# The second norm's sums, roots and reciprocals, moved some early products later in a hybrid layer's MLP

## The chip, the core and the metric

The kernel runs on one core of a Trainium2 chip. A core has a matrix engine (TensorE, PE in the rows), a vector engine (VectorE, DVE), a scalar engine (ScalarE, ACT), a general engine (GpSimd, POOL) and DMA queues that SyncE (SP) issues. Each engine works through its own list of instructions in order and waits where an operand or a buffer isn't ready. The metric is the device time of one execution in microseconds, the median of several runs.

## The reference

One decoder layer on 1024 positions of width 1024, all in float32. The mixer (convolution and retention heads) comes first; the change lies in what follows it, the squared-ReLU MLP under the second RMS norm:

```python
def rms_norm(x, g, eps=NORM_EPS):
    xf = x.astype(jnp.float32)
    y = xf * lax.rsqrt(jnp.mean(xf * xf, axis=-1, keepdims=True) + eps)
    return (y * g.astype(jnp.float32)).astype(x.dtype)

def sq_relu_mlp(u, w_up, w_down):
    hdn = jax.nn.relu(u @ w_up)
    return (hdn * hdn) @ w_down

    h = h + hybrid_mixer(rms_norm(h, norm1_g), w_in, conv_w, conv_norm_g, ret_norm_g, w_out)
    h = h + sq_relu_mlp(rms_norm(h, norm2_g), w_up, w_down)
```

## The kernel before

Everything is held transposed: features on the 128 partitions, tokens along the row, in two halves of 512 tokens (`hs[0]`, `hs[1]`). A float32 product is made of three faster ones: both factors are rounded to a high part (hi, on ACT) and the rest (lo, `tensor_sub`, on DVE), and hi times hi, hi times lo and lo times hi are added in one PSUM bank (`mm`). A weight piece comes as `r` by DMA, and `split_piece` makes `wh` on ACT and `wl` on DVE from it.

The up product is done by quadrants, with seven products in the place of eight. `MLP_ORDER = (1, 2, 6, 5, 3, 7, 4)` is the order of the seven kinds: kind 1 multiplies the quadrant "11" of the scaled x, 2 the quadrant "21", 3 the quadrant "22", and 5, 6, 7, 4 the sums of quadrants t1, t2, t3, t4. Each product is 12 matmuls (four pieces of 128 rows, three each) into a bank, which `Pair.take` then adds to others: kind 1 is copied out (ACT), kind 2 makes the result quadrant "11", kind 3 makes "12", and so on.

The second norm does not wait for its own root: x times the gain goes into the products, and the reciprocal root `r` of each token is multiplied in later, in `Pair.put`, as max(c, 0) * r on DVE, which a square on ACT follows. So `r` is first needed for the quadrant "11", made from kinds 1 and 2. It comes about in these parts: the squares of x are summed over feature blocks in `sums_[0]`, `sums_[1]` (ACT squares, POOL adds, while the mixer's last products run); a column of ones on PE sums them over partitions into a bank of tokens by 4 (`token_rnorms`, 8 matmul rows); ACT takes the root (a table load goes ahead of it); DVE takes the reciprocal and copies each value over 128 columns (`wide`); and PE multiplies that by the identity, so that each token's value stands on all partitions of a bank of the pool `pn` (`spread`). 

Between the mixer and the main loop stand 14 early products, for two pairs p = 0, 1 of feature groups: the loop near the end of the function runs over `at` = 0 to 13, which this text calls step 0 to 13 with product 0 to 13 (0 and 1 are kind 1 for the two pairs, 2 and 3 kind 2, 4 and 5 kind 6 on t2, 6 and 7 kind 5 on t1), and after each product come the preparation of a later weight piece (`prepare`, four steps ahead), the rest of the operands by a list written out by hand (`rest[at]`: `put_hi`, `put_lo`, the sums `sum4`, and so on), the squares put off by a step (`put_now`), and `take`. Before the change the ones' sums, the roots and the reciprocals are written at step 1, the spreading at step 3, and the `take` of product 2 is put off to step 3, behind the spreading. Pair 0 has two PSUM banks in turn (pool `pm`), pair 1 four (`pr`). The order in the code is the order on each engine.

After the early products the main loop runs over 7 blocks in which up products and down products alternate; a down product takes `V`, the hi and lo parts of the squared quadrants (`v_split`; the lo part of the second pair is POOL's).

Of the kernel before, what the change touches and what calls it, by code (L numbers as in the profile page):

```python
# [70 lines left out]
def hybrid_layer(  # L71
# [18 lines left out]
    dve = Engine(nc.vector, 1.18, now, clock)  # L90
# [26 lines left out]
    def tmp():  # L117
        return temps[-1].tile([P, H], F32, tag="t", name=nm("t"))

    def bank(pool_=None):  # L120
        return (pool_ or pm).tile([P, H], F32, tag="b", name=nm("b"))
# [47 lines left out]
    def prepare(n=1):  # L169
        for _ in range(n):  # L170
            if plan:
                part = plan.pop(0)()
                if part is None:
                    part = plan.pop(0)()
                parts.append(part)
# [105 lines left out]
    for i, t in enumerate(ropes):  # L281
        nc.sync.dma_start(t, rope[i])

    def token_rnorms(sums_, r, pool_=None):

        n = r.shape[-1]
        b = bank(pool_ or pr)
        for c in range(n):
            for i, q in enumerate(sums_):
                nc.tensor.matmul(  # L290
                    b[:, c : c + 1], q[:, c * P : (c + 1) * P], ones,
                    start=(i == 0), stop=(i == len(sums_) - 1),
                )
        act.activation(r, b[:, :n], AF.Sqrt, bias=eps, scale=1.0 / D)
        dve.reciprocal(r, r)
        wide = []
        for c in range(0, n, 4):
            m = min(n - c, 4)
            d = tmp()[:, : m * P].rearrange("p (a b) -> p a b", b=P)
            dve.tensor_copy(d, r[:, c : c + m, None].to_broadcast([P, m, P]))  # L300
            wide += [d[:, j] for j in range(m)]
        return wide

    def spread(wide, pool_=None):

        b = bank(pool_ or pr)[:, : len(wide) * P]
        for c, d in enumerate(wide):
            nc.tensor.matmul(b[:, c * P : (c + 1) * P], d, ident, start=True, stop=True)
        return b
# [4 lines left out]
    rtok = cp.tile([P, NC_], F32, name="rtok")  # L314
    zr = xp.tile([P, NH, NC_], F32, name="zr")
    for half in range(2):
        vb = [bank(pr if half else pm) for _ in range(4)]
        for k in range(KT):
# [11 lines left out]
            if half == 1 and k == 3:  # L330
                for c, sl in ((0, hs[0]), (4, hs[1])):
                    b = bank(pm)
# [17 lines left out]
        for i in range(4):  # L350
            c = half * 4 + i
# [351 lines left out]
    def put_hi(name, j, src):  # L703
        u = unit(F32R, "U")
        act.copy(u[:, :H], src)
        U.setdefault(name, [None] * 4)[j] = (u[:, :H], u[:, H:])

    def put_lo(name, j, src, eng=dve):
        hi, lo = U[name][j]
        eng.tensor_sub(lo, src, f32(hi))  # L710
# [129 lines left out]
    pn = ctx.enter_context(tc.tile_pool(name="pn", bufs=2, space=PSUM))  # L840
# [47 lines left out]
    sums_ = [tmp(), tmp()]  # L888
# [29 lines left out]
    def source(name, j):  # L918
        return un[j][:, hi_ if name == "t3" else lo_]
# [56 lines left out]
    todo = {}  # L976
# [47 lines left out]
    def put_now():  # L1024
        fs, later[:] = list(later), []
        for f in fs:
            f()

    def add(a, b):
        t = tmp()  # L1030
        dve.tensor_add(t, a, b)
        return t

    r_half = [None, None]

    class Pair:

# [13 lines left out]
        def take(self, n, b):  # L1051
            if n == 1:
                self.acc = tmp()
                act.copy(self.acc, b)
            if n == 2:
                self.put("11", add(self.acc, b))
            if n == 6:
                dve.tensor_add(self.acc, self.acc, b)
            if n == 5:
                self.both = add(self.acc, b)  # L1060
            if n == 3:
                self.put("12", add(self.both, b))
            if n == 7:
                dve.tensor_add(self.both, self.both, b)
                self.put("22", self.both)
                dve.tensor_add(self.acc, self.acc, b)
            if n == 4:
                dve.tensor_add(self.acc, self.acc, b)
                self.put("21", self.acc)
# [30 lines left out]
    early = [Pair((pm, pr)[p]) for p in range(EARLY)]  # L1100

    def hi(name, *js):
        return [lambda j=j: put_hi(name, j, source(name, j)) for j in js]

    def lo(name, eng, *js):
        return [lambda j=j: put_lo(name, j, source(name, j), eng) for j in js]

    def call(f, *js):
        return [lambda j=j: f(j) for j in js]
# [4 lines left out]
    def lo22(j):  # L1114
# [1 line left out]

    rest = [
        todo[32] + lo("t2", dve, 0, 1) + hi("t2", 2) + call(hi22, 0, 1),
        todo[33] + lo("t2", dve, 2) + todo[34] + hi("t2", 3) + call(lo22, 0, 1) + call(hi22, 2, 3),
        lo("t2", dve, 3) + hi("t3", 3) + call(lo22, 2, 3),  # L1120
        call(sum4, 0, 1) + hi("t4", 0, 1) + lo("t3", dve, 3),
        call(sum4, 2, 3) + hi("t4", 2, 3) + call(fetch_back, 0, 1, 2),
# [9 lines left out]
    ]  # L1132
    for at, (n, p) in enumerate((n, p) for n in MLP_ORDER for p in range(EARLY)):
        b = early[p].product(n)
        if at == 1:
            wides = [token_rnorms([sums_[h]], rtok[:, 4 * h : 4 * h + 4]) for h in range(2)]
            up.fetch(4)
        if at == 3:
            r_half[:] = [spread(w, pn) for w in wides]
        prepare()  # L1140
        for f in rest[at]:
            f()
        put_now()
        if at == 2:
            b2 = b
            continue
        if at == 3:
            early[0].take(n, b2)
        early[p].take(n, b)

    def down_product(n, h):
        hi, lo = parts.pop(0)
# [30 lines left out]
    def jobs(b, old, new):  # L1183

        todo = []
        for k, n in enumerate(DOWN_ORDER):
            four = [[] for _ in range(4)]
            if k < 6:
                for j in range(2):
                    four[j].append(lambda n=DOWN_ORDER[k + 1], j=j: v_split(old, n, j))  # L1190
                    four[j + 1].append(lambda n=DOWN_ORDER[k + 1], j=j: v_next(old, n, j))
            elif b < NBLK - 2:
                for j in range(2):
                    four[j].append(lambda j=j: v_both(new, 1, j))
            if b == NBLK - 2:
                late = {4: ((0, "11"), (0, "21"), (0, "12"), (0, "22")), 5: ((1, "11"),)}.get(k, ())
                for f, x in zip(four, late):
                    f.append(lambda x=x: last_split(*x))
                if k == 6:
                    for q in range(4):  # L1200
                        x = x2[2 * q + 1]
                        four[q].append(
                            lambda x=x: pool.tensor_add(x[:, hs[0]], x[:, hs[0]], x[:, hs[1]])
                        )
                    for f, name in ((four[0], "12"), (four[2], "22"), (four[3], "21")):
                        f.append(lambda name=name: last_split(1, name))
            todo += four
        return todo
# [4 lines left out]
    for b in range(NBLK - 1):  # L1213
        new = [Pair(pm), Pair(pm)]
        todo = jobs(b, pairs, new)
# [46 lines left out]
    for sl in (slice(0, 512), slice(512, 768), slice(768, 1024)):  # L1262
        n = sl.stop - sl.start
        G = T // n
        out = []
        for i in range(KT):
# [34 lines left out]
            if i == 2 and last:  # L1301
                wide = token_rnorms(*last[0])
            if i == 3 and last:
                finish(wide, *last[1])
            elif finishing:
                finishing.pop(0)()
        last = ([ssq3[:, sl], sq], rtok[:, sl.start // P : sl.stop // P]), (sl, out)
    finish(token_rnorms(*last[0]), *last[1], end=True)
    while finishing:
        finishing.pop(0)()  # L1310
# [96 lines left out]
```

## Time and profile before

| | |
|---|---|
| median of 3 runs | 1109.75 us (1109.44 to 1110.27) |
| the profiled execution: its own time | 1111.85 us |
| its span | 1110.0 us |
| PE busy | 1065.7 us, 96% of the span |
| DVE busy | 926.0 us, 83% |
| POOL busy | 578.1 us, 52% |
| ACT busy | 454.2 us, 41% |
| mean granted clock of PE | 0.982 |

The span is the time from the first to the last instruction of one profiled execution; 1.85 us of that execution's own time lie outside it. The profiled execution is 2.1 us above the median of the runs. An engine's busy share is a mean over stages, and a matmul counts as busy at either clock.

### The profile page before, as it was taken

How to read it: one execution, taken by the hardware profiler on the slowest of the kernel's cores; microseconds unless marked ns; L12 is line 12 of the kernel's file. 1: busy time of each engine (PE TensorE's matmuls, PEld its weight loads, DVE VectorE, ACT ScalarE, POOL GpSimd, SP SyncE). 2: the span in 40 equal slices, each digit the busy share in tenths (PEclk: the TensorE clock that was granted, in tenths of full speed). 3: DMA queues.
4: the chain of work that ended last, by engine and by line, in shares of the span. 5: the costliest groups of instructions: out<-in, count | busy, mean ns of one | idle time of the engine just before them, and what ended most of it. 6: DMA issues, size and time to landing. Idle time of an engine off the chain costs nothing.

```text
span 1110.0 us, 13715 instructions
## 1 busy us (share of the span) xinstructions
PE 1065.7 (96%) x4872; PEld 883.4 (80%) x4872; DVE 926.0 (83%) x1171; ACT 454.2 (41%) x817; POOL 578.1 (52%) x393
## 2 busy tenths in 40 slices
PE   7999999998798799989999999999999999999997
PEld 6778888887586588867788888888888888888886
DVE  8786486689999845579999989989989899899945
ACT  8211431456236433354344343433443343434453
POOL 6253234437776323536827629448267286284553
PEclk9999999999899899989999999999999999999998
DMA  7311112130111523032131120221211201200204
GB/s 266 143 57 48 30 39 75 49 142 16 36 46 46 199 86 124 1 100 71 48 96 29 49 86 29 67 58 39 79 37 58 86 29 48 86 20 19 70 9 152
DMA packets 38868, 76.68 MB, mean 69 GB/s; under 512 B 4368, under 2 KB 6416, under 8 KB 38800
## 3 DMA queue, kind: packets, MB, share of 16 engines
q1 hardware_dynamic: 38800, 75.80, 21.1%
q8 instruction: 39, 0.64, 0.2%
q14 instruction: 29, 0.24, 0.1%
HBM read 70.02 MB, written 5.77 MB: 68 GB/s over the span
## 4 chain that ended last, share of the span: by engine, by line
PE 77%; DVE 14%; issue 3%; DMA 2%; ACT 2%; POOL 1%; SPq 0%; DVEq 0%; POOLq 0%; ACTq 0%
PE b L361 49%; PE b L1159 22%; DVE wl L65 3%; PE b L323 2%; DVE U L65 1%; DVE t L65 1%; DVE r L65 1%; DVE z L65 1%; DVE xs L65 1%; DMA wv<-w_v 1%; DVE x L65 1%; DVE cv L65 1%; POOL r L65 1%; PE b L570 1%; PE b L538 1%
## 5 line engine op out<-in xcount | busy, mean ns | idle before, releaser
L65 ACT CAST wh<-r 128x512 fp32r<-128x512 f32 x286 | 176.7, 620 | 385.0 <-PE b L361 204.0
L361 PE MATMUL b<-U,wh 128*128 128x512 f32 x992 | 310.5, 394 | 8.5 <-DVE z L65 3.6
L65 DVE TENSOR_TENSOR wl<-r,wh 128x512 fp32r<-128x512 f32 x257 | 240.2, 937 | 76.1 <-ACT wh L65 75.2
L65 POOL TENSOR_TENSOR r<-r,r 128x512 f32<-128x512 f32 x136 | 210.2, 1548 | 131.6 <-DVE wl L65 79.6
L1159 PE MATMUL b<-V,wh 128*128 128x512 f32 x784 | 242.3, 390 | 1.1 <-POOL V L65 1.1
L361 PEld LDWEIGHTS b<-U,wh 128*128 128x128 f32 x992 | 188.4, 190 | 50.2 <-issue 4.4
L65 DVE TENSOR_TENSOR x<-x,b 128x512 f32<-128x512 f32 (+1 forms) x320 | 198.1, 665 | 28.7 <-PE b L361 28.7
L361 PE MATMUL b<-U,wl 128*128 128x512 f32 x496 | 195.3, 394 | 0.0
L1159 PEld LDWEIGHTS b<-V,wh 128*128 128x128 f32 x784 | 147.0, 188 | 33.1 <-POOL V L65 1.9
L65 POOL TENSOR_TENSOR t<-t,t 128x512 f32<-128x512 f32 x70 | 106.8, 1530 | 101.5 <-ACT t L65 55.4
L1159 PE MATMUL b<-V,wl 128*128 128x512 f32 x392 | 152.5, 389 | 0.0
L361 PE MATMUL b<-uh,wh 128*128 128x512 f32 x320 | 107.0, 399 | 4.3 <-DVE z L65 4.3
L361 PEld LDWEIGHTS b<-U,wl 128*128 128x128 f32 x496 | 94.5, 191 | 19.9
L361 PE MATMUL b<-uh,wl 128*128 128x512 f32 x320 | 105.6, 395 | 1.9 <-DVE wl L65 1.9
L361 PE MATMUL b<-ul,wh 128*128 128x512 f32 x320 | 105.9, 396 | 0.7 <-DVE ul L65 0.7
L65 POOL TENSOR_TENSOR wl<-r,wh 128x512 fp32r<-128x512 f32 x29 | 39.3, 1356 | 98.2 <-ACT wh L65 92.7
L1159 PEld LDWEIGHTS b<-V,wl 128*128 128x128 f32 x392 | 73.6, 188 | 15.2
L65 POOL TENSOR_TENSOR V<-t,V 128x512 fp32r<-128x512 f32 x35 | 49.1, 1402 | 67.2 <-ACT V L65 67.2
L65 DVE TENSOR_TENSOR t<-t,b 128x512 f32<-128x512 f32 x112 | 76.1, 680 | 1.7 <-POOL t L65 1.2
L65 ACT ACTIVATE t<-t 128x512 f32<-128x512 f32 x64 | 40.3, 631 | 84.6 <-DVE t L65 83.9
L361 PEld LDWEIGHTS b<-uh,wh 128*128 128x128 f32 x320 | 60.2, 192 | 17.6 <-issue 4.5
L361 PEld LDWEIGHTS b<-uh,wl 128*128 128x128 f32 x320 | 61.0, 191 | 15.3 <-DVE wl L65 2.4
(155 smaller groups left out, 1505.1 us busy)
## 6 DMA issues: line engine op xcount, KB each, us to landing
r<-w_up_t SPq DMA_DIRECT2D x64, 256.0 KB, 2.6
r<-w_down_t SPq DMA_DIRECT2D x56, 256.0 KB, 2.6
r<-w_in_t SPq DMA_DIRECT2D x48, 256.0 KB, 2.6
xt<-xT SPq DMA_DIRECT2D x16, 256.0 KB, 5.4
xs<-xT SPq DMA_DIRECT2D x8, 512.0 KB, 6.2
r<-w_out_t SPq DMA_DIRECT2D x16, 256.0 KB, 2.6
x<-xT SPq DMA_DIRECT2D x8, 512.0 KB, 8.8
rope<-rope SPq DMA_DIRECT2D x6, 512.0 KB, 6.8
```

Of the source, the lines that this page charges most:

```text
L65: return f(out, *args, **kw)
L323: nc.tensor.matmul(vb[i], a[k][:, tsl], b[k // 2][:, vs], start=(k == 0 and a is uh and b is vh), stop=(k == KT - 1 and a is ul),)
L361: nc.tensor.matmul(b, a[:, k, :], rhs(n, k)[r], start=(start and i == 0), stop=(stop and i == len(ops) - 1),)
L538: nc.tensor.matmul(bs[:, j * P : (j + 1) * P], k[j][:, sl], q[j][:, sl], start=True, stop=True)
L570: nc.tensor.matmul(bo[:, js], vj, sc[:, js], start=True, stop=(S is None))
L1159: nc.tensor.matmul(b, a, r, start=(i == 0), stop=(i == len(ops) - 1))
```

## The change

`token_rnorms` is cut into `token_roots` (ones' sums and roots) and `rnorms` (reciprocals and copies). In the loop over the early products the ones' sums and roots stand behind the `take` of product 3, the reciprocals behind that of product 5, the spreading behind that of product 6. Product 2 is taken at its own step; `take` then only adds, and the multiplying with `r` (`put` of the quadrant "11", one for each pair) is kept in `waiting` and done at steps 7 and 8. `up.fetch(4)` moves from step 1 to step 0. In step 1 of `rest` the two scaled hi parts of the quadrant "22" go ahead of the operand t2 of the last row block.

```diff
-    def token_rnorms(sums_, r, pool_=None):
+    def token_roots(sums_, r, pool_=None):
...
         act.activation(r, b[:, :n], AF.Sqrt, bias=eps, scale=1.0 / D)
+        return r
+
+    def rnorms(r):
+
+        n = r.shape[-1]
         dve.reciprocal(r, r)
         wide = []
...
             dve.tensor_copy(d, r[:, c : c + m, None].to_broadcast([P, m, P]))
             wide += [d[:, j] for j in range(m)]
         return wide
+
+    def token_rnorms(sums_, r, pool_=None):
+        return rnorms(token_roots(sums_, r, pool_))
...
-    r_half = [None, None]
+    r_half, waiting = [None, None], []
...
             if n == 2:
-                self.put("11", add(self.acc, b))
+                c = add(self.acc, b)
+                if r_half[0] is None:
+                    waiting.append(lambda: self.put("11", c))
+                else:
+                    self.put("11", c)
...
-        todo[33] + lo("t2", dve, 2) + todo[34] + hi("t2", 3) + call(lo22, 0, 1) + call(hi22, 2, 3),
+        todo[33] + lo("t2", dve, 2) + todo[34] + call(hi22, 2, 3) + hi("t2", 3) + call(lo22, 0, 1),
...
         b = early[p].product(n)
-        if at == 1:
-            wides = [token_rnorms([sums_[h]], rtok[:, 4 * h : 4 * h + 4]) for h in range(2)]
+        if at == 0:
             up.fetch(4)
-        if at == 3:
-            r_half[:] = [spread(w, pn) for w in wides]
         prepare()
         for f in rest[at]:
             f()
         put_now()
-        if at == 2:
-            b2 = b
-            continue
+        early[p].take(n, b)
         if at == 3:
-            early[0].take(n, b2)
-        early[p].take(n, b)
+            roots = [token_roots([sums_[h]], rtok[:, 4 * h : 4 * h + 4]) for h in range(2)]
+        if at == 5:
+            wides = [rnorms(r) for r in roots]
+        if at == 6:
+            r_half[:] = [spread(w, pn) for w in wides]
+        if at >= 7 and waiting:
+            waiting.pop(0)()
```

In DVE's list before, the reciprocals and copies (`rtok`, `t_3720`, `t_3729`) stand between the operands of step 0 (`un_3540`, `U_3641`, `U_3643`) and the first row of step 1 (`wl_3740`):

```order
L65 TENSOR_TENSOR un_3540<-un_3540 128x512
L65 TENSOR_TENSOR U_3641<-un_3049,U_3641 128x512
L65 TENSOR_TENSOR U_3643<-un_3208,U_3643 128x512
L65 RECIPROCAL rtok<-rtok 128x4
L65 COPY t_3720<-rtok 128x512
...
L65 COPY t_3729<-rtok 128x512
L65 TENSOR_TENSOR wl_3740<-r_3402,wh_3739 128x512
```

In the changed list they stand behind steps 1 to 5; these are its rows of steps 4 and 5 up to the first row of step 6 (`wl_3879`), with the sums of quadrants `un`, the operands t4 (`U_3786`, `U_3788`), and the takes of products 4 and 5 (`t_3706`, `t_3739`):

```order
L65 TENSOR_TENSOR wl_3819<-r_3232,wh_3818 128x512
L65 SCALAR_TENSOR_TENSOR un_3376<-x_2982,sm,un_3376 128x512
L65 SCALAR_TENSOR_TENSOR un_3540<-x_2983,sm,un_3540 128x512
L65 TENSOR_TENSOR t_3706<-t_3706,b_3805 128x512
L65 TENSOR_TENSOR wl_3851<-r_3404,wh_3850 128x512
L65 TENSOR_TENSOR U_3786<-un_3049,U_3786 128x512
L65 TENSOR_TENSOR U_3788<-un_3208,U_3788 128x512
L65 TENSOR_TENSOR t_3739<-t_3739,b_3837 128x512
L65 RECIPROCAL rtok<-rtok 128x4
L65 COPY t_3860<-rtok 128x512
...
L65 COPY t_3863<-rtok 128x512
L65 TENSOR_TENSOR wl_3879<-r_3234,wh_3878 128x512
```

The first reciprocal thus moves 25 rows of operands, weights and takes further back: from straight behind `U_3643`, the last row of step 0, to straight behind `t_3739`, the take of product 5.

In PE's list before, the ones' sums stand behind product 1 (`b_3700`) and the spreading behind product 3 (`b_3782`), ahead of product 4 (`b_3823`):

```order
L361 MATMUL b_3700<-U_3560,wl_3613 128x512
L290 MATMUL b_3713<-ones,t_3013 128x1 x4
L290 MATMUL b_3722<-ones,t_3014 128x1 x4
L361 MATMUL b_3759<-U_3111,wh_3629 128x512 x2
...
L361 MATMUL b_3782<-U_3597,wl_3658 128x512
L308 MATMUL b_3795<-ident,t_3720 128x128 x4
L308 MATMUL b_3800<-ident,t_3729 128x128 x4
L361 MATMUL b_3823<-U_3641,wh_3681 128x512 x2
```

In the changed list the sums stand behind product 3 (`b_3766`) and the spreading behind product 6 (`b_3865`), ahead of product 7 (`b_3897`):

```order
L369 MATMUL b_3766<-U_3597,wl_3658 128x512
L290 MATMUL b_3793<-ones,t_3013 128x1 x4
L290 MATMUL b_3799<-ones,t_3014 128x1 x4
L369 MATMUL b_3805<-U_3641,wh_3689 128x512 x2
...
L369 MATMUL b_3865<-U_3696,wl_3755 128x512
L316 MATMUL b_3887<-ident,t_3860 128x128 x4
L316 MATMUL b_3892<-ident,t_3863 128x128 x4
L369 MATMUL b_3897<-U_3190,wh_3779 128x512 x2
```

The sums move past two products and the spreading past three; no matmul is added or taken away.

In ACT's list the table load and the two roots now stand behind the casts of t4 of step 3 (`U_3786`, `U_3788`) and ahead of the weight cast of step 4:

```order
L65 CAST wh_3779<-r_3406 128x512
L65 CAST U_3786<-un_3049 128x512
L65 CAST U_3788<-un_3208 128x512
...
L65 ACTIVATE rtok<-b_3793,eps 128x4
L65 ACTIVATE rtok<-b_3799,eps 128x4
L65 CAST wh_3818<-r_3232 128x512
L65 CAST U_3826<-un_3376 128x512
```

Before, they stood behind the copy of product 0 and ahead of the weight cast of step 1; the table load itself is the row ahead of the first root in either list.

## Rows read from the trace of the kernel before

**Rows 1.** The chain of work that ended last, from the profile page: its share of the span by engine.

```profile
PE 77%; DVE 14%; issue 3%; DMA 2%; ACT 2%; POOL 1%; SPq 0%; DVEq 0%; POOLq 0%; ACTq 0%
```

**Rows 2.** The timeline of TensorE (PE) alone from the first early product on: start us, length us, then what ran; in brackets the idle time before it and who ended it. L361 are products of the halves, L290 the sums by the column of ones, L308 the spreading by the identity matrix. A product is 12 matmuls; 494.87 and 497.59 are the first rows of products 7 and 8.

```profile
463.48 0.62 PE L361 MATMUL b<-U,wh 128*128 128x512 f32 x2
...
468.92 0.95 PE L290 MATMUL b<-ones,t 128*128 128x1 f32 x8
470.81 1.05 PE L290 MATMUL b<-ones,t 128*128 128x1 f32 x8 [0.95 <-POOL t L65]
471.73 0.71 PE L361 MATMUL b<-U,wh 128*128 128x512 f32 x2
...
477.28 1.95 PE L308 MATMUL b<-ident,t 128*128 128x128 f32 x16
478.98 0.71 PE L361 MATMUL b<-U,wh 128*128 128x512 f32 x2
...
484.38 0.80 PE L361 MATMUL b<-U,wh 128*128 128x512 f32 x1 [2.87 <-DVE U L65]
...
492.06 0.70 PE L361 MATMUL b<-U,wh 128*128 128x512 f32 x2 [1.36 <-DVE t L65]
...
494.87 0.62 PE L361 MATMUL b<-U,wh 128*128 128x512 f32 x2
...
497.59 0.62 PE L361 MATMUL b<-U,wh 128*128 128x512 f32 x2
```

**Rows 3.** The timeline of ScalarE (ACT) alone over the same stretch: a COPY takes a product's bank, a CAST of wh<-r rounds a weight piece.

```profile
474.21 1.28 ACT L65 ACT_TABLE_LOAD   x1
...
475.81 0.62 ACT L65 CAST wh<-r 128x512 fp32r<-128x512 f32 x1
...
481.92 0.56 ACT L65 COPY t<-b 128x512 f32<-128x512 f32 x1
482.38 0.62 ACT L65 CAST wh<-r 128x512 fp32r<-128x512 f32 x1
```

**Rows 4.** The timeline of VectorE (DVE) alone there. wl rows finish a weight piece, U rows the lo half of an operand, un rows make sums of quadrants, t rows that read b take a product's bank. The row of 500.62 is the first of step 6.

```profile
475.80 0.18 DVE L65 RECIPROCAL rtok<-rtok 128x4 f32<-128x4 f32 x1 [3.29 <-ACT rtok L65]
...
476.91 0.69 DVE L65 TENSOR_TENSOR wl<-r,wh 128x512 fp32r<-128x512 f32 x1
...
479.38 0.75 DVE L65 SCALAR_TENSOR_TENSOR un<-x,sm,un 128x512 f32<-128x512 f32 x1
480.04 1.41 DVE L65 SCALAR_TENSOR_TENSOR U<-x,sm,U 128x512 fp32r<-128x512 f32 x2
483.03 0.69 DVE L65 TENSOR_TENSOR wl<-r,wh 128x512 fp32r<-128x512 f32 x1 [1.58 <-ACT wh L65]
483.64 0.68 DVE L65 TENSOR_TENSOR U<-un,U 128x512 fp32r<-128x512 f32 x1
484.24 2.43 DVE L65 SCALAR_TENSOR_TENSOR U<-x,sm,U 128x512 fp32r<-128x512 f32 x2
...
487.20 2.43 DVE L65 SCALAR_TENSOR_TENSOR un<-x,sm,un 128x512 f32<-128x512 f32 x2
489.55 1.77 DVE L65 TENSOR_TENSOR U<-un,U 128x512 fp32r<-128x512 f32 x1
491.24 0.68 DVE L65 TENSOR_TENSOR t<-t,b 128x512 f32<-128x512 f32 x1
...
493.95 0.69 DVE L65 TENSOR_TENSOR wl<-r,wh 128x512 fp32r<-128x512 f32 x1
...
500.62 0.68 DVE L65 TENSOR_TENSOR wl<-r,wh 128x512 fp32r<-128x512 f32 x1
```

**Rows 5.** The timeline of GpSimd (POOL) alone there (r rows work on raw weight pieces, x rows on the running x).

```profile
483.80 1.66 POOL L65 TENSOR_TENSOR r<-r,r 128x512 f32<-128x512 f32 x1 [13.04 <-DVE wl L65]
487.36 1.72 POOL L65 TENSOR_TENSOR r<-r,r 128x512 f32<-128x512 f32 x1 [1.90 <-DVE wl L65]
489.04 1.73 POOL L65 TENSOR_TENSOR x<-x,x 128x512 f32<-128x512 f32 x1
```

**Rows 6.** The timeline of PE alone in the first block of the main loop, columns as in rows 2; L1159 are the down products. The row of 516.63 begins the first down product, those of 520.32 and 554.01 begin up products, that of 550.29 a down product.

```profile
516.63 0.62 PE L1159 MATMUL b<-V,wh 128*128 128x512 f32 x2
...
518.37 0.50 PE L1159 MATMUL b<-V,wh 128*128 128x512 f32 x1 [0.67 <-POOL V L65]
...
520.32 0.62 PE L361 MATMUL b<-U,wh 128*128 128x512 f32 x2
...
550.29 0.70 PE L1159 MATMUL b<-V,wh 128*128 128x512 f32 x2
...
554.01 0.70 PE L361 MATMUL b<-U,wh 128*128 128x512 f32 x2 [0.71 <-ACT t L65]
```

**Rows 7.** Busy time by stretch of the whole core: start and end, length, then PE, PEld (weight loads), DVE, ACT, POOL busy with their instructions, the granted clock of PE (1.00 is 2.4 GHz, 0.50 is 1.2 GHz), share and rate of the DMA engines.

```profile
371.00:377.90 6.90, 2.94 (x7) 2.39 (x8) 6.81 (x10) 3.38 (x7) 1.64 (x1) 0.51 0.50 156
...
484.38:490.70 6.32, 6.32 (x14) 4.46 (x14) 6.32 (x6) 1.66 (x3) 4.42 (x3) 0.51 0.67 182
...
498.00:554.00 56.00, 54.62 (x239) 44.35 (x239) 54.30 (x73) 21.84 (x40) 39.77 (x26) 1.00 0.20 66
557.00:1075.00 518.00, 517.44 (x2292) 427.92 (x2290) 476.02 (x664) 210.81 (x366) 293.13 (x196) 1.00 0.17 52
```

**Rows 8.** The timeline of PE alone at the end of its longest earlier wait after the start, columns as in rows 2.

```profile
374.96 0.76 PE L361 MATMUL b<-yh,wh 128*128 128x512 f32 x1 [6.68 <-DVE z L65]
```

## Prediction

> **What bounds the kernel now.** I read the chain of work that ended last, then PE's own timeline where the change lies, then the engines it waits for there, then the stretch behind.
>
> The chain gives PE 77% and DVE 14% of the span [rows 1]. PE's busy share can't grow much: between 557 and 1075 us it is busy for 517.44 of 518.00 us [rows 7]. What is won or lost ahead of 557 us therefore moves the end one for one, and the question is when PE reaches that stretch.
>
> In the early products PE's timeline shows four losses [rows 2]. Two products take 463.48 to 468.92, so one takes 2.72. The ones' sums occupy 468.92 to 471.73, 2.81 us, of which 0.95 is a wait for POOL's last addition; 1.86 is work. Product 4 stops until 484.38 (a wait of 2.87) for the lo part of t2's last operand, from DVE. Product 6 stops until 492.06 (1.36) for the bank of product 2, whose take was put off. The spreading takes 477.28 to 478.98, 1.70, with no wait. Product 7 starts at 494.87 and ends at 497.59.
>
> Why is DVE late? It waits 3.29 us for the roots, until 475.80 [rows 4], because ACT loads a table from 474.21 and can round the next weight only at 475.81 [rows 3]. From then on DVE trails PE: it takes product 5 just ahead of 500.62 [rows 4], when PE has finished product 7. In 498 to 554 us DVE is busy for 54.30 of 56.00 us [rows 7], and its delay costs PE two more losses there [rows 6]: 516.63 to 520.32 is 3.69 for one product, 0.97 too much (the lo part of V, from POOL, which is held up by DVE's weight piece), and 550.29 to 554.01 is 3.72, 1.00 too much (ACT, behind DVE's take).
>
> **The change part by part.** No row is added on any engine; the cost is in the order, so I lay the rows of before out anew, engine by engine, with their own durations.
>
> *Sums and roots, removed from step 1.* PE runs products 0 to 3 through and then sums: 463.48 + 4 x 2.72 + 1.86 = 476.22. The 0.95 wait is gone. ACT rounds the weight of step 1 in the place of the table load, 474.21 + 0.62 = 474.83, and DVE's first row of step 1 starts at 474.85 where it was 476.91 [rows 3, 4]: 2.06 earlier.
>
> *Step 1 and the operand of product 4.* DVE's second sum of quadrants ended at 479.38 + 0.75 = 480.13, 3.22 behind that first row; now it ends at 478.07. On ACT an operand's cast (about 0.5), the copy (0.46, from 481.92 to 482.38) and the weight's cast (0.62) follow [rows 3]: 479.65. So DVE's row of 483.03 starts at about 479.70, 3.33 earlier. The moved hi parts of "22" fill time in which ACT waits for DVE anyway; without that cover they are two casts, and they sat ahead of this weight before. The late operand is ready at 483.64 + 0.68 - 3.33 = 480.99 [rows 4], so PE still stops in product 4, finishes it at about 481.5 (two matmuls of 0.23 remain), and products 5 and 6 end at 486.95 (up to 2.7 later if the clock falls over this stop, which the next wait hides). The bank of product 2 is taken in time now, so the 1.36 goes.
>
> *Where the wait goes.* Behind product 6 PE has the spreading, and that needs the copies which stand in DVE's list behind the take of product 5. Everything on PE behind it is held: product 7 and all later ones. So when does DVE get there?
> - From 483.03 to 491.24 the same rows took 8.21. Their slow ones are slow beside POOL: two operand rows in 484.24 to 486.60 and two sums in 487.20 to 489.55 take about 2.35 a pair against 1.41 for the pair of 480.04, and the row of 489.55 lasts 1.77 against 0.68; POOL's rows of 483.80, 487.36 and 489.04 run at that time [rows 4, 5]. They follow DVE's weight pieces, so they move with them. With one take (0.60) put in: 479.70 + 8.21 + 0.60 = 488.51; the take of product 3 makes it 489.11.
> - ACT's table load stands now behind the second sum (489.55 + 0.08 - 3.33 + 0.60 = 486.90), an operand's cast (0.5), then load and roots (474.21 to 475.81, 1.60) and the weight (0.62): 489.62. DVE goes on at 489.65.
> - Eight rows of steps 4 and 5 follow. Before, the same eight took 493.95 to 500.62, 6.67, with a wait for ACT inside; ACT has two operand casts of t4 in front of the weight now, too, so I take the 6.67: 496.32. Uncontended they would be about 5.
> - Reciprocal and copy of the first half: the two halves took 475.80 to 476.91, 1.11, so about 0.65 to the first copy's end: 497.0.
>
> So PE waits from 486.95 to 497.0, ten us. Spreading (1.70) and product 7 (2.72) give 501.4.
>
> *The clock.* After the wait of 6.68 us that ended at 374.96 the granted clock was 0.51 over 371.00 to 377.90, that is 1.2 GHz for 2.9 us after PE went on; after the stop that ended at 484.38 it was 0.51 to 490.70, some 6.2 us [rows 7, 8]. At half the clock half of that is lost: 1.5 to 3.1 us, middle 2.3. In before it was hidden, since product 6 waited for the bank; here PE has nothing else to wait for and pays it. Product 7 ends at 503.7 against 497.59 [rows 2]: 6.1 later (5.3 to 6.9).
>
> *What comes back.* DVE does not lose as much: behind the copies it has a few rows of steps 6 and 7 and then waits for product 7. So it no longer trails PE, and the two losses of 0.97 and 1.00 [rows 6] go: 6.1 - 1.97 = 4.1. `up.fetch(4)` one step earlier costs nothing, as its pieces are first rounded at step 10; the deferred multiplications with r are needed by V at step 12 and by DVE alone, in the time that it waits for PE.
>
> The sum against the profiled execution is 1111.85 + 4.1 = 1115.95; that one lies 2.1 above the median, and I put the difference on the median: 1109.75 + 4.1 = 1113.9.
>
> *A rule against a row.* The table load lasts 1.28 us [rows 3]. The Trainium skill, page "ScalarE: Activation LUTs", Terms, gives about 2.7 us for copying a table set into the active tables. By that the roots' place on ACT would hold DVE 1.4 us more and the sum would be 5.5; by the row it stays at 4.1, and the row decides.
>
> **Bounds.** Downwards: DVE without any delay beside POOL or behind ACT: 25 rows from 474.85 at 0.61 (483.03 to 483.64) and 0.65 are 490.8; then product 7 ends at 497.5, level with before, and with both later losses gone the change is -2.1; with the clock's loss at 1.5, -2.9. Upwards: 6.9 with none of the later losses gone, and one us more for DVE: 7.9. I stand near the upper rows for DVE's path, since the same rows took that long beside the same POOL rows.
>
> **The rivals.**
> - *About level: DVE is partly freed.* POOL's rows could fall elsewhere, since DVE's takes of products 2 and 3 now lie singly between the others. If half of the five us of delay goes, the copy is ready at 494.5 and the change is +1.6: 1111.4. For it: such a take stands in the list between the rows that were slow beside POOL. Against it: POOL's rows follow DVE's weights and keep their distance. 0.20.
> - *Faster.* All of the delay goes: 1106.9 to 1107.7. It decides where the first copy ends at 492.9: from there 4.42 and 2.3 of clock reach 499.6, just the 1.97 that come back. That is four us ahead of my sum. If the clock also stays at 2.4 GHz the point is 495.1. 0.10.
> - *The later losses stay.* POOL and DVE are loaded as before in 498 to 554 [rows 7], and the V of the first down product may still come late: +6.1, 1115.9. Against it: DVE then has waited for PE for some us. 0.15.
> - *The forecast*, 1113.9, own range 1112.5 to 1115.5: 0.55.
>
> **How the numbers follow.** I count 0.2%, 2.2 us, as about what a measurement of this kernel can tell from no change. The forecast and the staying losses lie above it, 0.70; the level case lies within it, with a little of the others: 0.20; the rest, 0.10, is faster. The range reaches over the level case down to 1109.3 and up to 1117.3 (7.5 above, near the upper bound).
>
> **What would show it.** Right: one long wait of PE ahead of the spreading of about ten us, on DVE's copy, with the clock at 1.2 GHz behind it; a shorter stop in product 4, near two us; no wait ahead of product 6, and none in the first block of the main loop; DVE's reciprocals near 496. Wrong: the copy ending ahead of 493, the wait short, or PE at 2.4 GHz straight behind it; or stops in the first block as long as before.

## The result, and the profile after

The changed kernel takes 1114.68 us (median of 6 runs, 1113.4 to 1115.18) against 1110.25 us for the kernel before (6 runs, 1109.44 to 1110.54): ratio 1.0039, interval 1.0027 to 1.0052. That is 4.43 us slower (3.0 to 5.8 by the interval); 4.1 were forecast. The profiled execution has a time of 1114.82 and a span of 1113.0 us, 3.0 longer than the span of before. The profiled execution of before lay 1.6 above its median and this one 0.14, so this pair of traces shows 3.0 of the 4.43.

The chain that ended last, from the page after: PE's share rose from 77 to 82%, DVE's fell from 14 to 11% [rows 1].

```profile
PE 82%; DVE 11%; issue 3%; ACT 2%; DMA 0%; POOL 0%; SPq 0%; DVEq 0%; POOLq 0%; ACTq 0%
```

All waits of PE from 440 to 580 us of the kernel after: line, what it waited for, us in total, how often, the longest.

```profile
PE b L316 <- DVE t L65: 9.9, 1, 9.9
PE b L369 <- DVE U L65: 1.8, 1, 1.8
PE b L369 <- ACT U L65: 0.3, 1, 0.3
```

The same for the kernel before:

```profile
PE b L361 <- DVE U L65: 2.9, 1, 2.9
PE b L361 <- DVE t L65: 1.4, 1, 1.4
PE b L290 <- POOL t L65: 0.9, 1, 0.9
PE b L361 <- ACT t L65: 0.7, 1, 0.7
PE b L1159 <- POOL V L65: 0.7, 1, 0.7
```

Five waits, 6.6 us together, became three, 12.0 together. What stopped PE for the bank, for POOL's t, for V and for ACT's t is gone; in its place stands one wait of the spreading (L316) for DVE's copy. PE's timeline after, with the columns of [rows 2]; L369 are products of the halves:

```profile
463.09 0.62 PE L369 MATMUL b<-U,wh 128*128 128x512 f32 x2
...
473.97 1.84 PE L290 MATMUL b<-ones,t 128*128 128x1 f32 x16
...
480.62 0.50 PE L369 MATMUL b<-U,wh 128*128 128x512 f32 x1 [1.83 <-DVE U L65]
...
496.74 3.78 PE L316 MATMUL b<-ident,t 128*128 128x128 f32 x16 [9.89 <-DVE t L65]
500.17 0.82 PE L369 MATMUL b<-U,wh 128*128 128x512 f32 x2
...
503.12 0.62 PE L369 MATMUL b<-U,wh 128*128 128x512 f32 x2
```

The row of 503.12 is the first of product 8, and so the end of product 7. Product 0 starts 0.39 us earlier than in before (463.09 against 463.48), ahead of all that the change moves, so 0.39 is added where places of the two are compared. But for the two stops in product 4 (0.3 and 1.8 us in the list of waits), sums and products 4 to 6 follow each other up to 486.85, then PE stands for 9.89 us.

DVE's timeline after, over the wait, with the columns of [rows 4]:

```profile
484.03 2.44 DVE L65 SCALAR_TENSOR_TENSOR un<-x,sm,un 128x512 f32<-128x512 f32 x2
486.40 1.76 DVE L65 TENSOR_TENSOR U<-un,U 128x512 fp32r<-128x512 f32 x1
...
489.40 1.65 DVE L65 TENSOR_TENSOR wl<-r,wh 128x512 fp32r<-128x512 f32 x1 [0.64 <-ACT wh L65]
...
493.58 0.76 DVE L65 TENSOR_TENSOR wl<-r,wh 128x512 fp32r<-128x512 f32 x1 [0.61 <-ACT wh L65]
...
496.06 0.16 DVE L65 RECIPROCAL rtok<-rtok 128x4 f32<-128x4 f32 x1
496.26 0.43 DVE L65 COPY t<-rtok 128x512 f32<-128x512 f32 x1
...
503.81 0.69 DVE L65 TENSOR_TENSOR wl<-r,wh 128x512 fp32r<-128x512 f32 x1 [4.78 <-ACT wh L65]
```

But for two waits of 0.6 us for ACT, DVE works until its first copy ends at 496.69; 0.05 later PE starts. Behind the copies DVE runs out of work and stands for 4.78 us: it no longer trails PE. The busy times by stretch after, with the columns of [rows 7]:

```profile
486.70:496.74 10.04, 0.15 (x2) 0.00 (x1) 8.76 (x13) 4.91 (x9) 5.07 (x4) 0.67 0.54 195
496.74:500.20 3.46, 3.46 (x17) 3.46 (x17) 2.25 (x5) 0.00 (x0) 0.39 (x1) 0.50 0.50 192
500.20:503.00 2.80, 2.80 (x14) 2.34 (x14) 0.00 (x0) 0.00 (x0) 2.80 (x3) 0.96 0.03 10
503.00:557.00 54.00, 54.00 (x240) 44.72 (x239) 49.60 (x68) 22.40 (x40) 35.68 (x24) 1.00 0.14 39
```

The spreading runs at 0.50, 1.2 GHz, and takes 3.43 us (496.74 to 500.17) where it took 1.70 in before; product 7 is back at 2.4 GHz all but its start (0.96) and takes 2.95 (500.17 to 503.12) in the place of 2.72. From 503 to 557 PE is busy all the time.

### The profile page after: what moved, and what is told of

Read it like the earlier page. It is cut to its first block, busy times and chain, and to the rows that moved or that the text cites. A ratio compares the mean times of both kernels' runs of the same rounds, so it can differ in the third digit from the quotient of the medians.

```text
span 1113.0 us, 13717 instructions
## 1 busy us (share of the span) xinstructions
PE 1063.8 (96%) x4872; PEld 883.0 (79%) x4872; DVE 926.2 (83%) x1171; ACT 454.3 (41%) x817; POOL 576.6 (52%) x393
## 4 chain that ended last, share of the span: by engine, by line
PE 82%; DVE 11%; issue 3%; ACT 2%; DMA 0%; POOL 0%; SPq 0%; DVEq 0%; POOLq 0%; ACTq 0%
PE b L369 53%; PE b L1171 23%; PE b L331 2%; DVE wl L65 2%; DVE r L65 1%; DVE z L65 1%; DVE xs L65 1%; DVE U L65 1%; DVE cv L65 1%; DVE ul L65 1%; PE b L578 1%; PE b L546 1%; DVE un L65 1%; PE b L586 1%; PE b L580 1%
## 5 line engine op out<-in xcount | busy, mean ns | idle before, releaser
L369 PE MATMUL b<-U,wh 128*128 128x512 f32 x992 | 308.5, 392 | 5.7 <-DVE z L65 3.6
L65 DVE TENSOR_TENSOR wl<-r,wh 128x512 fp32r<-128x512 f32 x257 | 237.4, 927 | 84.1 <-ACT wh L65 82.7
L369 PEld LDWEIGHTS b<-U,wh 128*128 128x128 f32 x992 | 187.5, 189 | 46.2 <-issue 2.3
L369 PE MATMUL b<-U,wl 128*128 128x512 f32 x496 | 194.2, 391 | 0.0
L369 PE MATMUL b<-uh,wh 128*128 128x512 f32 x320 | 107.0, 399 | 4.4 <-DVE z L65 4.3
L369 PEld LDWEIGHTS b<-U,wl 128*128 128x128 f32 x496 | 93.8, 189 | 19.8
L369 PE MATMUL b<-uh,wl 128*128 128x512 f32 x320 | 105.7, 395 | 1.9 <-DVE wl L65 1.9
L369 PE MATMUL b<-ul,wh 128*128 128x512 f32 x320 | 105.9, 396 | 0.7 <-DVE ul L65 0.7
L369 PEld LDWEIGHTS b<-uh,wh 128*128 128x128 f32 x320 | 60.2, 192 | 17.6 <-issue 4.5
L369 PEld LDWEIGHTS b<-uh,wl 128*128 128x128 f32 x320 | 61.0, 191 | 15.3 <-DVE wl L65 2.4
L369 PEld LDWEIGHTS b<-ul,wh 128*128 128x128 f32 x320 | 60.9, 190 | 14.6 <-DVE ul L65 1.6
```

The lines of the kernel that those rows point to most:

```text
L65: return f(out, *args, **kw)
L369: nc.tensor.matmul(b, a[:, k, :], rhs(n, k)[r], start=(start and i == 0), stop=(stop and i == len(ops) - 1),)
```

## The experiments

The theory: PE waits for copies that stand late in DVE's list; what this costs is the wait, plus the slow clock behind it, less the later losses that vanish since DVE is no longer behind. The first rival: it is the new order on DVE (takes, multiplications with r) that costs the time, wherever the spreading stands. The second: the clock costs little, and the wait alone is the loss. E1 to e4 ran together (before: 1109.97 us there), and e5 to e8 (before: 1109.9).

**e1: the spreading two products later, all else as in the changed kernel.**

```diff
+        if at == 8:
+            r_half[:] = [spread(w, pn) for w in wides]
         early[p].take(n, b)
 ...
-        if at == 6:
-            r_half[:] = [spread(w, pn) for w in wides]
-        if at >= 7 and waiting:
+        if at >= 8 and waiting:
```

> The changed kernel with the spreading placed behind product 8 in the place of product 6 (ahead of that product's take, which needs r); DVE's reciprocals stay where the change put them. Theory (the loss is PE's wait ahead of the spreading for DVE's copy, at about 496.7): products 7 and 8 run inside that wait, delayed by 2.1 us and 1.3 us for the banks of products 3 and 4, the wait ahead of the spreading shrinks from 9.9 us to about 1 us, product 9 starts 1.5 to 1.9 us earlier than in the kernel before, and as DVE too is some 1.8 us ahead of before, the time is 1108.4 us (1107.5 to 1109.5), 6 us below the changed kernel and below the kernel before. Rival (the loss comes from DVE's and ACT's order, the late table load and the late takes): these stay, so the time stays near 1114.5.

Measured: 1108.81 us, ratio 0.9986 (0.9977 to 0.9995): 1.2 below the kernel before and, with each set against the kernel before that ran with it, 5.6 below the changed kernel. PE's timeline in e1, its four waits of over half a microsecond up to the spreading:

```profile
478.44 0.66 PE L369 MATMUL b<-U,wh 128*128 128x512 f32 x1 [1.82 <-DVE U L65]
...
486.74 0.70 PE L369 MATMUL b<-U,wh 128*128 128x512 f32 x2 [0.51 <-ACT rtok L65]
...
491.00 0.70 PE L369 MATMUL b<-U,wh 128*128 128x512 f32 x2 [1.26 <-ACT U L65]
494.65 2.05 PE L316 MATMUL b<-ident,t 128*128 128x128 f32 x16 [0.64 <-DVE t L65]
```

This execution runs 2.18 earlier than the one after (the stop in product 4 ends at 478.44 against 480.62), so its spreading starts at 496.83 in the times of after: the copies are as late as they were. PE has done products 7 and 8 in the meantime and waits 0.64 instead of 9.89. (The waits of 0.51 and 1.26 ahead of these two products are put down to ACT; by order and time they are for the banks of products 3 and 4, which DVE's takes free, as e8 shows for the second.) DVE's list is the same up to the copies, so the first rival falls: the place in PE's list is what costs.

**e2: the spreading where the change has it, on data that are there early** (it leaves out the scale of the second norm).

```diff
+    ready = [[ident] * 4] * 2
 ...
-            r_half[:] = [spread(w, pn) for w in wides]
+            r_half[:] = [spread(w, pn) for w in ready]
```

> The changed kernel with the spreading in its place behind product 6, but made from the identity matrix, which is ready from the start, in the place of DVE's copies; DVE still makes reciprocals and copies. So r is 1 and the second norm's scale is left out of the hidden values. Theory: PE has no wait ahead of the spreading; product 7 waits to 488.8 for the bank of product 3, product 8 to 493.0 for that of product 4, and from there DVE is the bound, which stands where it does in the changed kernel, some 1.8 us ahead of the kernel before: 1108.3 us (1107.3 to 1109.5). Rival (DVE's or ACT's order is to blame): 1114.5.

Measured: 1107.6 us, ratio 0.9981 (0.9972 to 0.9989). PE's timeline: the spreading has no wait, and others come back behind it.

```profile
488.17 1.95 PE L316 MATMUL b<-ident 128*128 128x128 f32 x16
...
494.69 0.70 PE L369 MATMUL b<-U,wh 128*128 128x512 f32 x2 [1.24 <-ACT U L65]
...
516.59 0.50 PE L1172 MATMUL b<-V,wh 128*128 128x512 f32 x1 [1.02 <-POOL V L65]
```

With PE not held, DVE is behind again, and the loss at the first down product is there, as in before [rows 6]. Both halves of the theory, the wait and what comes back, show in this one run.

**e3 and e5: matmuls without use ahead of the spreading**, 36 and 42 of them, to keep PE from standing.

```diff
         if at == 6:
+            warm = bank(pn)
+            for i in range(36):        # 42 in e5
+                nc.tensor.matmul(
+                    warm, U["11"][i % 4][0][:, :P], U["11"][i % 4][0], start=True, stop=True
+                )
             r_half[:] = [spread(w, pn) for w in wides]
```

> The changed kernel with 36 matmuls of 128x512 on an operand that is ready (about 8.2 us), into a bank of the pool pn, put between product 6 and the spreading, that is inside PE's wait of 9.9 us. Theory: the granted clock stays at 2.4 GHz, the spreading takes 1.7 us in the place of 3.4, and the time falls by that: 1112.9 us (1112.3 to 1113.6). Rival (the clock's part is nothing, or the spreading's 3.4 us come from its operands): 1114.6, no change against the changed kernel; if the matmuls overrun the wait, above 1114.6.

> As the kernel with 36 matmuls ahead of the spreading, with 42 of them (about 9.5 us), so that PE's wait behind them is about 0.4 us in the place of 1.9 us. Theory (the clock falls because PE waits, and costs 1.7 us in the spreading): the granted clock stays at 1.00 through the spreading, which takes 1.7 us, and the time is 1112.9 us (1112.3 to 1113.6) against about 1114.6 for the change. Rival (the spreading is slow for another reason): the spreading takes 3.3 us again at 0.5, and the time is 1114.6.

Measured: e3 1113.04 (ratio 1.0026, 1.0016 to 1.0035), e5 1112.44 (1.0021, 1.0012 to 1.0030). PE's timeline in e3, and then the busy times by stretch (columns of [rows 7]) over its spreading:

```profile
488.65 8.32 PE L1161 MATMUL b<-U 128*128 128x512 f32 x36
498.88 3.63 PE L316 MATMUL b<-ident,t 128*128 128x128 f32 x16 [1.91 <-DVE t L65]
```

```profile
498.88:502.30 3.42, 3.42 (x17) 3.42 (x17) 2.25 (x5) 0.00 (x0) 0.74 (x1) 0.53 0.71 224
```

In e3 1.91 us of wait are left, and the clock fell to 0.53 all the same; so this trace doesn't tell the clock from the wait. It is also of e3's slowest execution (1116.87), so that the median of 1113.04, as expected, is not explained by it. In e5 the matmuls reach over the copy. PE's timeline, DVE's first copy, and the busy times:

```profile
489.87 9.68 PE L1161 MATMUL b<-U 128*128 128x512 f32 x42
499.39 1.95 PE L316 MATMUL b<-ident,t 128*128 128x128 f32 x16
...
501.10 0.71 PE L369 MATMUL b<-U,wh 128*128 128x512 f32 x2
```

```profile
498.01 0.43 DVE L65 COPY t<-rtok 128x512 f32<-128x512 f32 x1
```

```profile
499.00:503.00 4.00, 4.00 (x27) 3.61 (x26) 1.78 (x3) 0.00 (x0) 2.78 (x3) 1.00 0.43 139
```

Here PE never stands behind product 6, the clock is 1.00, and the spreading takes 1.71 us (499.39 to 501.10) instead of 3.43: 1.7 us are the clock's, and the second rival falls. By the medians the clock's part is about 1.9 (e5 is 2.5 us slower than the kernel before, 1.3 to 3.3, and the changed kernel 4.4). This trace, of e5's slowest execution, shows less of that in the end (649.1 us from product 0 on, against 649.9 after), since its matmuls run 0.95 us over the copy's end at 498.44. The other 2.5 are what the wait costs with the clock kept up.

**e4: the kernel before, and in it only the take of product 2 put back in its turn.**

```diff
         if at == 2:
-            b2 = b
+            c2 = add(early[0].acc, b)
             continue
         if at == 3:
-            early[0].take(n, b2)
+            early[0].put("11", c2)
```

> The kernel before with one part of the change alone: the take of product 2 (the addition) at its own step 2; the multiplication with r stays behind the spreading at step 3. Theory (DVE is the bound from step 3 to 554 us, so a wait of PE taken away there comes back later): the wait of 1.36 us ahead of product 6 goes, but the waits at the first down product and at 554 us grow by as much: 1110.2 us, within 0.4 of the kernel before. Rival (PE's waits add up, each removed one is a gain): 1108.9.

Measured: 1110.26 us, ratio 1.0003 (0.9994 to 1.0012): no difference. PE's timeline in e4, at product 4 and at the start of product 8:

```profile
481.27 0.79 PE L361 MATMUL b<-U,wh 128*128 128x512 f32 x1 [2.85 <-DVE U L65]
...
493.85 0.74 PE L361 MATMUL b<-U,wh 128*128 128x512 f32 x2 [2.35 <-DVE t L65]
```

The 1.36 ahead of product 6 [rows 2] is gone, and 2.35 stands ahead of product 8, again for DVE's t. The time is as expected; the place is not: the wait comes back there and not at the first down product, whose 0.67 is gone too. While DVE is behind PE, a wait that is taken away came back at a later thing that DVE owes.

**e6: four of POOL's subtractions, `new_basis` 5 and 7, two and three steps later**, behind those that wait for a DMA.

```diff
-        call(new_basis, 5),
-        call(new_basis, 7),
-        call(new_basis, 3),
+        [],
+        [],
+        call(new_basis, 3),
+        call(new_basis, 5, 7),
```

> The changed kernel with POOL's four subtractions on the running x (new_basis 5 and 7) written at step 11 in the place of steps 8 and 9, so that they stand behind those of step 10, which wait for a transfer until about 499.8 us, and no longer run beside DVE's rows of steps 3 to 5. Theory (DVE's rows on two SBUF operands wait while POOL runs): the row of 1.76 us at 486.40 falls to 0.68, but DVE then waits for ACT's weight until 489.40 all the same; the row of 1.65 at 489.40 falls to 0.69 and the rest of steps 4 and 5 comes 1.0 us earlier; the first copy ends at 495.7 in the place of 496.7 and the time falls by 1.0 us, to 1113.6 (1112.9 to 1114.3). Rival (POOL's rows have no part in DVE's delay): 1114.6 and the same rows of DVE.

Measured: 1113.57 us, ratio 1.0034 (1.0021 to 1.0047). DVE's timeline in e6, with the rows that answer to those of 486.40 and 489.40 after, and PE's:

```profile
485.15 0.68 DVE L65 TENSOR_TENSOR U<-un,U 128x512 fp32r<-128x512 f32 x1
...
488.15 0.69 DVE L65 TENSOR_TENSOR wl<-r,wh 128x512 fp32r<-128x512 f32 x1 [1.72 <-ACT wh L65]
```

```profile
494.46 3.78 PE L316 MATMUL b<-ident,t 128*128 128x128 f32 x16 [8.91 <-DVE t L65]
```

Without POOL beside them the two rows last 0.68 and 0.69 instead of 1.76 and 1.65. Of these 2.04 us 1.08 go into a longer wait for ACT (1.72 instead of 0.64), and 0.98 reaches PE. So POOL does slow these rows, as the prediction had it, and about half of what they delay is hidden behind ACT. What the 0.98 are worth at the end is not settled: in this execution product 7 started at 1.2 GHz too (0.75 over 497.92 to 500.72), and from product 0 on the trace takes as long as the one after (650.0 us against 649.9); by the medians e6 is 0.8 closer to the kernel before than the changed kernel is, which is within their intervals.

**e7: reciprocals and copies one step earlier on DVE.**

```diff
-        if at == 5:
+        if at == 4:
             wides = [rnorms(r) for r in roots]
```

> The changed kernel with the reciprocals and copies one step earlier on DVE, behind the take of product 4; the spreading stays behind product 6. Theory (the end follows the time of DVE's first copy one for one as long as PE waits there): the copy ends at about 493.5 in the place of 496.7, PE's wait is 6.7 us in the place of 9.9, and the time is 1111.4 us (1110.7 to 1112.3). Rival (the loss hangs on the spreading's place in PE's list alone): 1114.6; rival (the later stretch takes up the gain): above 1113.

Measured: 1111.14 us, ratio 1.0011 (1.0002 to 1.0020). DVE's timeline in e7 at the first copy, POOL's beside it, and PE's at the wait:

```profile
492.52 0.98 DVE L65 COPY t<-rtok 128x512 f32<-128x512 f32 x1
```

```profile
491.95 1.26 POOL L65 TENSOR_TENSOR x<-x 128x512 f32<-128x512 f32 x1 [2.02 <-DVE un L65]
```

```profile
493.56 3.48 PE L316 MATMUL b<-ident,t 128*128 128x128 f32 x16 [7.33 <-DVE t L65]
```

The wait shrinks by 2.56 instead of 3.2: the copy lies now beside a row of POOL's and lasts 0.98 instead of 0.43. The time is as expected and neither rival's: as long as PE waits there, the end follows DVE's copy.

**e8: roots at step 2, reciprocals at step 3, spreading at step 7.**

```diff
-        if at == 3:
+        if at == 2:
             roots = ...
-        if at == 5:
+        if at == 3:
             wides = [rnorms(r) for r in roots]
-        if at == 6:
+        if at == 7:
             r_half[:] = [spread(w, pn) for w in wides]
```

> The changed kernel with sums and roots behind the take of product 2 (where ACT is idle), reciprocals behind that of product 3, the spreading behind product 7. Theory: the table load no longer holds DVE (0.64 us), PE finds the copies nearly ready (at about 489.4) and waits at most 0.3 us ahead of the spreading, then some 1.3 us for the bank of product 4; DVE is the bound to 554 us and stands 2.4 us ahead of the kernel before, and PE waits again in the first block: 1107.8 us (1106.8 to 1108.8), level with or just below the kernel with the spreading at step 8. Rival (PE's waits add up): 1105.5 or less.

Measured: 1106.9 us, ratio 0.9972 (0.9961 to 0.9982): 3.0 us faster than the kernel before and, each against its own kernel before, 7.4 faster than the changed kernel. PE's timeline in e8, and two rows of DVE's:

```profile
487.81 1.16 PE L316 MATMUL b<-ident,t 128*128 128x128 f32 x8 [0.16 <-DVE t L65]
489.22 1.16 PE L316 MATMUL b<-ident,t 128*128 128x128 f32 x8 [0.25 <-DVE t L65]
491.83 0.69 PE L369 MATMUL b<-U,wh 128*128 128x512 f32 x2 [1.46 <-ACT U L65]
...
513.05 0.50 PE L1171 MATMUL b<-V,wh 128*128 128x512 f32 x1 [0.99 <-POOL V L65]
```

```profile
487.87 1.29 DVE L65 COPY t<-rtok 128x512 f32<-128x512 f32 x1
...
491.01 0.67 DVE L65 TENSOR_TENSOR t<-t,b 128x512 f32<-128x512 f32 x1
```

The spreading waits 0.41 us in all. The 1.46 ahead of product 8 are put down to ACT's U, but the casts that end there are of t4, and product 8 multiplies "22". What it needs is the bank of product 4, and DVE's take of that product, the row of 491.01, ends in the same moment (491.68). At the first down product PE waits for V again. So DVE is the bound here, as it is in before. The earlier `up.fetch(4)` and the moved hi parts of "22" are in e8 as in the changed kernel, so they are not the loss.

How the stretch moved, from the starts of product 0 and of the first down product in each trace, and from there to the span's end (before: 463.48, 516.63 and 1110.0; after: 463.09, 522.16 and 1113.0):

| kernel | product 0 to first down product | from there to the end |
|---|---|---|
| before | 53.15 | 593.4 |
| after | 59.07 | 590.8 |
| e1 | 51.97 | 592.5 |
| e2 | 49.89 | 593.4 |
| e3 | 59.11 | 590.9 |
| e4 | 54.22 | 592.1 |
| e5 | 58.23 | 590.9 |
| e6 | 58.63 | 591.4 |
| e7 | 56.18 | 590.9 |
| e8 | 49.80 | 593.3 |

Where PE was held ahead of the spreading (after, e3, e5, e6, e7) the rest takes some 591 us, elsewhere 592 to 593.4: in the changed kernel 2.5 us of before are given back, since DVE got time to catch up.

## Why the prediction was right

**DVE's path.** The forecast laid DVE's rows out anew to a copy that ends at 497.0. It ended at 496.69, which is 497.08 with the 0.39. The steps on the way fit as well: the weight row of step 2 was put at 479.70 and came at 479.66, the lo part that product 4 waits for at 480.99 and came at 480.95, the weight row behind the table load at 489.65 and came at 489.79 (all with the 0.39). The slow rows kept their place beside POOL, which the level rival denied: two pairs of 2.44, and 1.76. The 6.67 taken over for the last eight rows came out as 6.66 (489.40 to 496.06), but by luck. In before those 6.67 held a wait of 1.66 for ACT:

```profile
498.21 0.69 DVE L65 TENSOR_TENSOR wl<-r,wh 128x512 fp32r<-128x512 f32 x1 [1.66 <-ACT wh L65]
```

After, that wait is 0.61 (the row of 493.58), 1.05 less, and the weight row of 489.40, which took 0.69 in before, lasts 1.65 beside POOL, 0.96 more. The prediction foresaw neither.

**The table load.** ACT's timeline after:

```profile
487.14 1.28 ACT L65 ACT_TABLE_LOAD   x1
```

It lasted 1.28 again, and the wait came out at 9.89, not at the 11.4 that the 1.4 us more of a 2.7 us load would have made of the ten. The row decided rightly over the figure of the Trainium skill, page "ScalarE: Activation LUTs", Terms.

**PE's wait.** "Ten us" were 9.89; the stop in product 4 "near two" was 1.83; that ahead of product 6 is gone.

**The clock.** The price was put at 1.5 to 3.1 us, middle 2.3. It was about 2.0: 1.73 in the spreading, which ran at 1.2 GHz, and 0.23 in product 7. With that product 7 ends at 503.51 (503.12 and the 0.39) instead of the forecast 503.7, 5.9 later than before and not 6.1. The upper figure rested on the 6.2 us at the low clock in before [rows 7], and that was no guide to this place.

**What comes back.** 1.97 were forecast from the two losses of [rows 6], and both waits are gone. From the end of product 7 to the span's end before takes 612.41 us (1110.0 less 497.59) and after 609.88 (1113.0 less 503.12): 2.53 came back, 0.56 more than forecast. The two errors have the same sign, so the pair of traces shows 5.9 - 2.5 = 3.4 for the change where the sum says 4.1 (and 3.0 between the spans, with the 0.39 ahead of product 0). The medians differ by 4.43. Where the rest lies is open; the traces of the ten kernels start product 0 between 460.38 and 465.09 us, so one pair settles no single microsecond. The mechanism is shown; that the sum lies within 0.4 us of the medians' difference is luck in part, since the terms as traced give 3.4.

## What to carry to other kernels

TensorE takes its list in order: a matmul that needs a lagging engine's result holds everything behind it (here product 7, for 9.89 us), so it belongs where that engine's result is there, and not where its own user wants it; two products later it waited 0.64 us here, and the kernel was 5.6 us faster. Before such a move, lay the lagging engine's rows out one by one with their own durations, the slow ones too: this gave the place of the copy to 0.1 us, though two errors of one us cancelled in it. And count what the lagging engine gains in the time that the other stands, since here it gave 2.5 of 5.9 us back.

## What the runs showed of the hardware that was not expected

- The clock after a stop can't be read off the stop's length. The same stop of 1.82 to 1.83 us in product 4, behind the same list on PE, was followed by 1.2 GHz in e1 (0.58 over 478 to 482) and not in the changed kernel (1.00 over 480.62 to 484.62), as the busy times by stretch show, e1's first:

```profile
478.00:482.00 4.00, 3.56 (x9) 2.79 (x10) 4.00 (x6) 0.10 (x1) 1.52 (x1) 0.58 0.24 66
```

```profile
480.62:484.62 4.00, 4.00 (x17) 3.29 (x18) 4.00 (x5) 0.00 (x0) 1.51 (x2) 1.00 0.17 66
```

- DVE's copy of one small SBUF operand is slowed beside POOL as well, not only rows with two full SBUF operands: 0.43 us alone, 0.98 in e7 and 1.29 in e8. Rows that read a bank keep 0.67 to 0.69 in the traces of before, after, e1, e6 and e8 from 462 to 580 us.
